# Thirty-five inner tiles of three feed-forward halves made with seven half-size products in place of eight

## The chip, the cores and the metric

The kernel runs on one core of one Trainium2 chip, in a single launch. The metric is the device time of an execution in microseconds, the median of three runs. All inputs come from the chip's memory, and packing of the inputs on the host is not timed.

## The reference, cut to what matters

A two-layer transformer over two token streams of 256 tokens each: a context stream and a latent stream, 1024 features. Each layer has a feed-forward half, a mixer (recurrence, two kinds of attention) and a second feed-forward half. A feed-forward half is, with 2816 inner features,

```
n   = rms_norm(h) * scale + shift            # 1024 features, scale and shift from a product with w_mod
gu  = n @ w_in                               # 2 x 2816: gate and up
h   = h + 0.5 * g * ((silu(gate) * up) @ w_out)
```

It is done for both streams with the same weights (each stream has its own scale, shift and g), except that the last layer's second half is done for the latent stream alone. So there are three halves over 512 tokens and one over 256. The vectors scale, shift and g come from w_mod (1024 x 9216 per layer) times a vector per stream. All is float32.

## The kernel before, in words

**Products.** Features lie on the 128 partitions, tokens along the free axis: x is eight tiles of 128 x 512, columns 0 to 255 the context, 256 to 511 the latents. To keep float32 precision, each operand is split in a high part in the rounded type fp32r and a low part (the rest), and a product is three matmuls: high by high, high by low, low by high (`mm3`, L625, its matmuls on L628 to L630). The normalised input is held in XH and XL.

**Weights.** All weights are packed by the host in the order of use into chunks of eight 128 x 128 blocks (128 x 1024, 512 KB; `plan`, L54). `loader` (L606) brings a chunk into a `raw` buffer (3 of them); ScalarE makes the high part (`split_hi`, L334) and VectorE the low part (`split_lo`, L340) into a pair of the `ring` (5 pairs). A raw buffer is free after the low part, a ring pair after the chunk's last matmul.

**A feed-forward half** (`ffn`, L813). There are 22 inner tiles f of 128 features. For each, gate and up are made over 8 tiles of k: 16 blocks, each three matmuls of 512 columns, into two PSUM banks (L898 to L905). `evac` (L825) then gives SiLU of gate on ScalarE (L830), the product with up on VectorE (L834), and the split of the result on ScalarE and VectorE (L846, L857). The first two or three tiles are made together, k by k, while the input is still being normalised. Inner tiles are taken in two groups of 11 (`GF`): after a group, `contract` (L908) multiplies its 11 tiles by w_out for each of the eight output tiles, three matmuls of 512 columns for each pair, and VectorE adds the result to x (`add_out`, L804, once for each stream).

**The modulation vectors.** While a feed-forward half runs, VectorE also forms the next scales, shifts and gates as dot products: `gemv` (L670) fetches 128 rows of w_mod (512 KB into a `graw` buffer, 6 of them) and takes two dot products over 1024 elements (L680, with an accumulator read behind each). `pump` (L702) lets a given number (`rates`) of them into the queue after each inner tile and output tile.

**The order of the work.** Every engine's instruction order is written out when the kernel is built. `Weave` (L362) is a planner: each piece of work is a step with an engine, a cost, buffers that it takes and gives, events that it waits for and an urgency; the planner always places the step that can start first, and of those within a small slack the one with the smallest urgency number. Dot products have urgency 90 (`U_GEMV`), the weight splits 18 (`U_W`), the evacuation of inner tiles 12 (`U_EVAC`). On the chip each engine follows its list in order and waits for the semaphores of what it needs. The lists `RANK`, `START`, `INPUTS` and `ORDER` set urgencies and order in the two mixers and at the start of the kernel, where the first scales and shifts are made by dot products (L1707) and small matmuls (L1691) from rows fetched in the order of `INPUTS`.

Of the kernel before, what the change touches and what calls it, by code (L numbers as in the profile page):

```python
# [17 lines left out]
try:  # L18
# [11 lines left out]
KT = 8  # L30
NF = FF // 128
GF = NF // 2
EPS = 1e-6
CH = 8
# [5 lines left out]
ORDER = ((("lx", 1), ("ukv", 0), ("nq", 0), ("nv", 0), ("lx", 2), ("cq", 0), ("cq", 1),  # L40
# [12 lines left out]

def plan():  # L54

    out = []

    def ffn(l, w):
        first = 3 if (l, w) == (0, 1) else 2
        for k in range(KT):  # L60
            out.extend((("fi", l, w, f, up, k), 1) for f in range(first) for up in range(2))
        for g in range(2):
            for f in range(max(first, g * GF), (g + 1) * GF):
                for up in range(2):
                    out.extend((("fi", l, w, f, up, k), 1) for k in range(KT))
            for dts in out_tiles(l, w):
                out.extend((("fo", l, w, dt, f), 1) for f in range(g * GF, (g + 1) * GF) for dt in dts)
# [24 lines left out]
def uses(key):  # L92

    kind, l = key[0], key[1]
    lat = l == L - 1
    if kind == "fi":
        _, _, w, f, _, _ = key
        return 2 if f < 2 and (l, w) != (0, 1) and not (lat and w == 2) else 1
    if kind == "fo":
        _, _, w, dt, f = key  # L100
        return 2 if f >= GF and dt >= KT - NORM_DT["ffn"] and not (lat and w == 2) else 1
# [26 lines left out]
def pack_weights(a):  # L128
    def block(key):
        kind, l = key[0], key[1]  # L130
        if kind == "fi":
            _, _, w, f, up, k = key
            m = a["ffn%d_w_in" % w][l]
            return m[k * 128:(k + 1) * 128, up * FF + f * 128:up * FF + (f + 1) * 128]
        if kind == "fo":
            _, _, w, dt, f = key
            return a["ffn%d_w_out" % w][l][f * 128:(f + 1) * 128, dt * 128:(dt + 1) * 128]
# [166 lines left out]
class Stream:  # L304
# [36 lines left out]

    def get(self, key):
# [19 lines left out]
class Weave:  # L362
# [62 lines left out]
    def run(self):  # L425
        while self.programs:
# [36 lines left out]
U_W, U_MAIN, U_EVAC, U_GEMV = 18, 50, 12, 90  # L463
N_POOL = 6
RANK = ({"ckv": 19.2, "conv": (-2, 47.5, 37.5), "nk": (-0.7, 19), "nv": 2.5, "cq": 16.9,
         "nq": (23, 10.2), "values": 72.2, "keys": (8, 17, 43.6),
         "query": (35.2, 45.9, 4.5, 18.5, 4.2, 11.8), "lru": (40, 40, 41), "gelu": (25, 22, 29),
         "att": (31, 11, 24.9, 17, 35), "evac": (50.4, 13.4, 5.8, 14.5, 32.1),
         "pv": (18.5, 13.5, 26.5, 34.1, 21.5), "main": 50},
        {"ckv": 48.7, "conv": (8, 38, 29), "nk": (36.5, 19.1), "nv": 43.7, "cq": 14.1, "nq": (7, 2),  # L470
         "values": 61.7, "keys": (18, 10, 19), "query": (9.5, -2.5, 10.5, 8.5, 7.7, 43.8),
         "lru": (40, 40, 43), "gelu": (16.8, 9.5, 32), "att": (25.6, 4, 2, 8, 49.2),
         "evac": (14, 23, 48.5, 17, 45.2), "pv": (9.5, 26.5, 8.5, 12.5, 13.5), "main": 50})
U_WNEXT, N_NEXT = 20, 9
START = {"scale": (1, 11, 5, 24.5, 29.2, 3, 9, 16),
         "shift": (24.6, 9.8, 8, 13, 29.8, 41.6, 14, 6.6),
         "apply": (0.5, 0.6, -1.5, -5.5, -5.5, -5.5, 1.5, -6.5)}
INPUTS = (("x", 1), ("x", 0), ("x", 2), ("cst",), ("x", 3), ("x", 4), ("x", 5), ("x", 6), ("x", 7),
          ("cols",), ("mod", 0, 0), ("weights", 1), ("mod", 1, 0), ("weights", 0), ("mod", 0, 1),
          ("mod", 1, 2), ("mod", 1, 1), ("mod", 0, 2), ("mod", 1, 3), ("weights", 2), ("mod", 0, 7),  # L480
          ("mod", 0, 3), ("mod", 1, 4), ("mod", 0, 5), ("mod", 0, 4), ("weights", 3), ("weights", 5),
          ("weights", 4), ("mod", 1, 5), ("mod", 0, 6), ("mod", 1, 6), ("mod", 1, 7))
# [4 lines left out]
def emit(tc, xT, cc, wmod, wst, cols_d, cst_d, nab, gates, wm0, ccol, out, layers=L):  # L487
# [3 lines left out]
    with es:  # L491
# [5 lines left out]
        raw = pool("raw", 3)  # L497
        ring = pool("ring", 5)
# [7 lines left out]
        w = Weave(dict(mm=3, sc=2, tr=2, o=1, ring=5, raw=3, nsq=2, nt=2), W)  # L506
# [104 lines left out]
        def split_hi(cs):  # L611
            for c in cs:
                yield S("ACT", act(W.size(c)), lambda: W.split_hi(c), take={"ring": 1},
                        wait=[("raw", c)] + ([("hi", c - 1)] if c else []), fire=("hi", c))

        def split_lo(cs):
            for c in cs:
                n = W.size(c)
                yield S(("DVE", "POOL") if c < N_POOL else ("DVE",), (dve(n), 2.3), lambda e=None: W.split_lo(
                    c, G if e == "POOL" else V), wait=[("hi", c)], give={"raw": 1}, fire=("chunk", c))  # L620

# [24 lines left out]
        def open_ffn():  # L646
            st = ph["st"] = ExitStack()
            ph["h"] = pool("ffnh", GF, st)
            ph["t"] = pool("ffnt", 2, st)
            ph["g"] = pool("gemv", 6, st)  # L650
            ph["g1"] = pool("gemv1", 1, st)
            now = w.clock["PE"]
            for tag, n in (("hp", GF), ("sg", 2), ("h", 2), ("graw", 6)):
                w.free[tag] = [now] * n
            ph["n"] = ph.get("n", 0) + 1
            if queue and ph["n"] > 1:
                w.spawn(U_GEMV - 1, silu_c(), now)
# [44 lines left out]
        def pump(n):  # L702
            for _ in range(min(n, len(queue))):
# [109 lines left out]
        def ffn(l, ww, p, streams, nxt, rates, start):  # L813
# [63 lines left out]

            if not both:
                w.spawn(1, rows(), w.clock["PE"])

# [16 lines left out]
            for grp in range(2):  # L897
                for f in range(max(done, grp * GF), (grp + 1) * GF):  # L898
# [7 lines left out]
                fs = range(grp * GF, (grp + 1) * GF)  # L906
# [45 lines left out]
        def mixer(l, p):  # L952
# [354 lines left out]
            def both_heads(a, s, i, evs, last):  # L1307
# [12 lines left out]
                yield S("PE", 1.4 * keys / 512, score, take={"sc": 2}, wait=[("nk", j), ("nq", j)] + evs["s"],  # L1320
# [292 lines left out]
        def startup():  # L1613
# [11 lines left out]

            def fetch(c, k):
                def f():
                    r = rows[c, k] = ph["g"].tile([128, 1024], F32, name="graw")
                    nc.sync.dma_start(r, wm0[ON_PE.index((c, k))] if (c, k) in ON_PE else wmod[0, c * 8 + k])
                return load(1024, f, take={"graw": 1}, fire=("wm", c, k))  # L1630

            def inputs():
                yield load(16, lambda: nc.sync.dma_start(sil[:, :, :2], ccol), fire="sil0")
                for s in range(2):
                    def row():
                        crow.append(ph["g"].tile([128, 1024], F32, name="graw"))
                        nc.sync.dma_start(crow[s][:1, :], cc[s * 1024:(s + 1) * 1024].unsqueeze(0))
                    yield load(3, row, take={"graw": 1}, fire=("crow", s))
# [19 lines left out]
            def wide(s, i):  # L1658
# [6 lines left out]
                yield S("PE", 0.86, copies, idle=True, take={"mm": 1}, give={"graw": 1} if i else {}, wait=[("crow", s)])  # L1665
# [16 lines left out]
            def product(c, k):  # L1682
# [13 lines left out]
                yield S("PE", 0.67, prod, idle=True, take={"sc": 1}, give={"graw": 1}, wait=[("wm", c, k), "sil"])  # L1696
# [6 lines left out]
            def dots(c, k):  # L1703

                m = mod[0, c][:, :, k]
                for s in range(2):
                    yield S("DVE", 1.14, lambda: V.scalar_tensor_tensor(  # L1707
                        ph["junk"], rows[c, k], 1.0, ph["sc"][:, s, :], OP.mult, OP.mult, accum_out=m[:, s:s + 1]),
                        wait=[("wm", c, k), ("silc", ph["n"], s)], give={"graw": 1} if s else {})
# [46 lines left out]
        def main():  # L1756
# [3 lines left out]
            yield from ffn(0, 1, 0, (0, 1), (0, 3), (2, 1), True)  # L1760
# [5 lines left out]
            yield from ffn(0, 2, 2, (0, 1), (1, 0), (2, 1), False)  # L1766
# [3 lines left out]
            yield from ffn(1, 1, 3, (0, 1), (1, 3), (2, 1), False)  # L1770
# [34 lines left out]
```

## Time and profile before

| what | value |
|---|---|
| median of 3 runs | 1765.95 us (1765.78 to 1766.14) |
| the profiled execution's own time | 1765.4 us |
| its span in the trace | 1763.6 us |
| PE busy / DVE busy / ACT busy | 1729.3 / 1194.7 / 694.9 us |
| bytes read from memory | 249.10 MB |

PE is TensorE's matmuls, PEld its weight loads, DVE VectorE, ACT ScalarE, POOL GpSimd, SPq the queue from which all transfers are issued. Matmuls are pipelined, and each record is longer than the distance to the next start; so the pace of a stream is read from starts, not from durations. A VectorE record likewise reaches some 0.08 us into the next one when the engine has no gap.

### The profile page before, as it was taken

What the parts mean: (1) busy time and instruction counts of PE and PEld (TensorE: products, weight loads), DVE (VectorE), ACT (ScalarE), POOL (GpSimd) and SP (SyncE); (2) the same over time, 40 slices, a digit from 0 to 9 for tenths busy, and PEclk for the clock granted to TensorE, in tenths of its full rate; (3) what the DMA queues carried; (4) which work ended last, traced back from release to release, by engine and by line L of the source; (5) the groups of instructions that cost most, each with busy time, mean ns of one, the idle gap of its engine ahead of it and who ended that gap; (6) DMA issues with size and microseconds to landing.
All of it is one profiled execution on the core that took longest, in us unless ns stands there. A gap on an engine that the chain in (4) does not pass through costs nothing.

```text
span 1763.6 us, 24185 instructions
## 1 busy us (share of the span) xinstructions
PE 1729.3 (98%) x9508; PEld 1428.9 (81%) x9508; DVE 1194.7 (68%) x1960; ACT 694.9 (39%) x1092; POOL 83.5 (5%) x70
## 2 busy tenths in 40 slices
PE   7999999999999999999999999999999999899999
PEld 4788888889766798888888898888888976599999
DVE  6898677636778678776775488765334577777564
ACT  4432122224777653222222242212222377754442
POOL 1100000000111010000000100000000111110000
PEclk9999999999999999999999999999999999999999
DMA  8565455322221126554553255543222232145554
GB/s 321 194 202 179 167 180 189 136 93 92 76 72 52 37 96 230 188 179 155 191 191 114 101 179 191 188 161 140 96 96 96 77 98 78 60 143 181 182 183 123
DMA packets 73591, 251.74 MB, mean 143 GB/s; under 512 B 9090, under 2 KB 12418, under 8 KB 73220
## 3 DMA queue, kind: packets, MB, share of 16 engines
q1 hardware_dynamic: 73476, 250.18, 41.4%
q8 instruction: 75, 1.23, 0.3%
q14 instruction: 40, 0.33, 0.1%
HBM read 249.10 MB, written 1.05 MB: 142 GB/s over the span
## 4 chain that ended last, share of the span: by engine, by line
PE 92%; DVE 4%; ACT 2%; issue 1%; POOL 0%; DMA 0%; SPq 0%; POOLq 0%; ACTq 0%; DVEq 0%
PE mm L628 27%; PE mm L629 27%; PE mm L630 27%; PE tr L1274 1%; PE sc L1298 1%; PE o L1351 1%; PE mm L1413 1%; DVE junk L1707 1%; PE o L628 1%; PE o L630 1%; PE o L629 1%; PE sc L1008 1%; PE tr L949 1%; PE sc L1316 1%; PE sc L628 0%
## 5 line engine op out<-in xcount | busy, mean ns | idle before, releaser
L628 PE MATMUL mm<-xh,whi 128*128 128x512 f32 (+2 forms) x1722 | 625.4, 363 | 8.7 <-DVE xh L990 5.2
L629 PE MATMUL mm<-xl,whi 128*128 128x512 f32 (+2 forms) x1722 | 613.8, 356 | 0.8 <-DVE xl L771 0.8
L630 PE MATMUL mm<-xh,wlo 128*128 128x512 f32 (+2 forms) x1722 | 613.3, 356 | 0.0
L334 ACT CAST whi<-wraw 128x1024 fp32r<-128x1024 f32 (+1 forms) x316 | 330.4, 1046 | 667.9 <-PE mm L629 458.9
L340 DVE TENSOR_TENSOR wlo<-wraw,whi 128x1024 fp32r<-128x1024 f32 (+1 forms) x311 | 379.5, 1221 | 256.2 <-ACT whi L334 253.3
L628 PEld LDWEIGHTS mm<-xh,whi 128*128 128x128 f32 x1722 | 326.4, 190 | 66.3 <-issue 6.9
L629 PEld LDWEIGHTS mm<-xl,whi 128*128 128x128 f32 x1722 | 326.4, 190 | 52.0 <-issue 2.6
L630 PEld LDWEIGHTS mm<-xh,wlo 128*128 128x128 f32 x1722 | 326.1, 189 | 50.6
L680 DVE SCALAR_TENSOR_TENSOR junk<-graw,silc 128x1024 f32<-128x1024 f32 x256 | 312.7, 1221 | 6.6 <-DMA graw<-in_wmod_dram 2.2
L628 PE MATMUL mm<-hh,whi 128*128 128x512 f32 (+1 forms) x748 | 264.5, 354 | 0.0
L629 PE MATMUL mm<-hl,whi 128*128 128x512 f32 (+1 forms) x748 | 263.2, 352 | 0.0
L630 PE MATMUL mm<-hh,wlo 128*128 128x512 f32 (+1 forms) x748 | 262.5, 351 | 0.0
L628 PEld LDWEIGHTS mm<-hh,whi 128*128 128x128 f32 x748 | 140.7, 188 | 21.3
L630 PEld LDWEIGHTS mm<-hh,wlo 128*128 128x128 f32 x748 | 140.4, 188 | 21.6
L629 PEld LDWEIGHTS mm<-hl,whi 128*128 128x128 f32 x748 | 140.8, 188 | 20.5
L804 DVE SCALAR_TENSOR_TENSOR x<-mm,mod,x 128x256 f32<-128x256 f32 x158 | 71.2, 479 | 86.0 <-PE mm L630 85.5
L846 ACT CAST hh<-h 128x512 fp32r<-128x512 f32 (+1 forms) x88 | 49.6, 567 | 158.1 <-DVE h L834 133.8
L834 DVE TENSOR_TENSOR h<-sg,mm 128x512 f32<-128x512 f32 x62 | 42.5, 686 | 69.8 <-PE mm L630 69.1
L857 DVE TENSOR_TENSOR hl<-h,hh 128x512 fp32r<-128x512 f32 (+1 forms) x88 | 54.5, 623 | 33.9 <-ACT hh L846 33.7
L723 POOL TENSOR_TENSOR acc<-acc,nsq 128x256 f32<-128x256 f32 x20 | 20.5, 1023 | 1097.3 <-ACT nsq L719 1097.3
L743 POOL TENSOR_TENSOR rr<-rv,nhalf 128x2 f32<-128x2 f32 (+2 forms) x29 | 37.8, 1308 | 289.8 <-DVE rv L736 212.7
L719 ACT ACTIVATE nsq<-x 128x256 f32<-128x256 f32 x63 | 25.5, 415 | 62.2 <-DVE x L804 62.2
(240 smaller groups left out, 1508.1 us busy)
## 6 DMA issues: line engine op xcount, KB each, us to landing
wraw<-in_wst_dram SPq DMA_DIRECT2D x308, 512.0 KB, 3.5
graw<-in_wmod_dram SPq DMA_DIRECT2D x137, 512.0 KB, 5.2
graw<-in_wm_dram SPq DMA_DIRECT2D x7, 512.0 KB, 7.2
x<-in_xT_dram SPq DMA_DIRECT2D x8, 256.0 KB, 5.0
nab<-in_nab_dram SPq DMA_DIRECT2D x16, 128.0 KB, 2.1
silc<-in_cc_dram SPq DMA_DIRECT2D x2, 1024.0 KB, 5.9
m_gw<-in_gates_dram SPq DMA_DIRECT2D x6, 256.0 KB, 3.6
out_dram<-x SPq DMA_DIRECT2D x8, 128.0 KB, 1.9
```

The source lines that it names most:

```text
L334: self.nc.scalar.copy(hi[:, :n], self.raws[i][:, :n])
L340: eng.tensor_tensor(lo[:, :n], self.raws.pop(i)[:, :n], hi[:, :n].bitcast(F32), OP.subtract)
L628: PE.matmul(o, wh[:, :m], h, start=start, stop=False)
L629: PE.matmul(o, wh[:, :m], lo, start=False, stop=False)
L630: PE.matmul(o, wl[:, :m], h, start=False, stop=stop)
L680: V.scalar_tensor_tensor(ph["junk"], g["r"], 1.0, ph["sc"][:, s, :], OP.mult, OP.mult, accum_out=mod[l, c][:, s, j:j + 1])
L719: A.activation(t, x[:, dt, half(s)], AF.Square)
L743: G.tensor_tensor(r, v, e, OP.pow)
L804: yield S("DVE", 0.4, lambda: V.scalar_tensor_tensor(x[:, dt, half(s)], o[:, half(s)], gate[:, s, dt:dt + 1], x[:, dt, half(s)], OP.mult, ...
L834: V.tensor_tensor(g["h"][:, cs], g["s"][:, cs], pu[:, cs], OP.mult)
L846: A.copy(hs[f][0][:, cs], g["h"][:, hc])
L857: yield S("DVE", dve(n), lambda: V.tensor_tensor(hs[f][1][:, cs], g["h"][:, hc], hs[f][0][:, cs].bitcast(F32), OP.subtract), give={"h": 1} ...
```

## The change

In 35 of the 66 inner tiles of the three halves over both streams, gate and up are made by the Winograd form of a two by two block product. The weights of a tile are the blocks gate and up by k 0 to 3 and k 4 to 7; the input's blocks are k 0 to 3 and k 4 to 7 by context and latents. Seven products of half-size blocks (four k tiles, 256 columns) take the place of eight. Each product is 4 k tiles by three matmuls of 256 columns. The tiles: `DIRECT` gives the first such f of each half, 13, 12 and 6; so 9, 10 and 16 tiles.

- **Weights of such a tile** (`seven`): its two chunks hold the four blocks (`sa`, `sb`). VectorE forms four sums of blocks over 512 elements, and of the seven resulting operands ScalarE makes the high parts (three over 512 elements, two over 1024) and VectorE the low parts (the same five). They lie in three ring pairs and a half-size pair (`half`); one scratch tile `sx`.
- **Input sums** (`sums_of_x`, `last_sum`): once for each half, six sums and three splits over 1024 elements, and for each of four k tiles three sums and a split over 256. The last of them overwrites a quarter of XH and XL when the plain tiles are done. Two `graw` buffers and `sx` serve as scratch.
- **Products** (`fast`, `fasts`): products 1, 5, then 3 of the tile before, 6, 2, 4 of the tile before, 7; at the end of a group 3 and 4 of its last tile. They accumulate in quarters of three PSUM banks.
- **Evacuation** (`evac7`): ScalarE copies three partial results (256 columns), applies SiLU twice (256) and makes the high part (512); VectorE adds twice, multiplies twice (256 each) and makes the low part (512).
- **Groups**: the three halves have three groups of inner tiles (8, 7, 7) in place of two of 11; the fourth half keeps two of 11.
- **Buffers**: raw 3 to 4, ring 5 to 6, graw 6 to 2 in the three halves; the rows for the start lie in a pool of their own (`graw0`, 6) that is closed before the input sums.
- **Lists**: `RANK`, `START`, `INPUTS`, `ORDER` and the numbers of `pump` (`RATES`, now fractions) have other values; the planner's cost of the scores of one mixer step is another; `dynamic_dma_scratch_size=1024` is given.

```diff
-GF = NF // 2
+GROUPS = {(0, 1): (0, 8, 15, 22), (0, 2): (0, 8, 15, 22), (1, 1): (0, 8, 15, 22), (1, 2): (0, 11, 22)}
+DIRECT = {(0, 1): 13, (0, 2): 12, (1, 1): 6, (1, 2): 22}
...
+URG = {'seven': 16.7, 'evac7': -10.7, 'sums': (24.4, 52.7, 10.8), 'last': 4.6}
+RATES = ((4.11, 1.93, 2.03), (2.3, 0.51, 2.05), (1.04, 0.93, 1.42))
...
-        raw = pool("raw", 3)
-        ring = pool("ring", 5)
+        raw = pool("raw", 4)
+        ring = pool("ring", 6)
...
+                yield S("ACT", act(512), open_a, take={"ring": 1}, wait=[("raw", c), ("hi", c - 1) if begins else
+                                                                         other(-1, "openC")], fire=ev("openA"))
+                yield S("DVE", dve(512), lambda: lo("A", a, raw(0, a)), fire=ev("A11"))
+                yield S("DVE", dve(512), s3, take={"sx": 1})
+                yield S("DVE", dve(512), s1, wait=[("raw", c + 1)], fire=ev("s1"))
+                yield S("DVE", dve(512), lambda: tt(g["x"][:, b], raw(0, b), raw(0, a), OP.subtract), fire=ev("s2"))
...
+                yield S("ACT", act(1024), open_c, take={"ring": 1}, wait=[] if begins else [other(-1, "openB")],
+                        fire=ev("openC"))
+                yield S("DVE", dve(1024), lambda: lo("C", whole, g["x"]), wait=[ev("s4")], give={"sx": 1},
+                        fire=ev("C"))
...
+                yield S("DVE", dve(512), lambda: tt(raw(0, a), raw(1, b), g["x"][:, b], OP.subtract), fire=ev("s4"))
+                yield S("ACT", act(512), lambda: hi("A", b, raw(0, b)))
+                yield S("DVE", dve(512), lambda: lo("A", b, raw(0, b)), fire=ev("S1"))
+                yield S("ACT", act(512), open_d, take={"half": 1})
+                yield S("DVE", dve(512), lambda: lo("D", a, raw(0, a)), give={"raw": 1}, fire=ev("D"))
...
+                yield S("ACT", act(1024), open_b, take={"ring": 1}, wait=[ev("s1"), ev("openC") if ends else
+                                                                          other(1, "openA")], fire=ev("openB"))
...
+                yield S("DVE", dve(1024), lambda: lo("B", whole, raw(1, whole)), give={"raw": 1}, wait=[ev("s4")],
+                        fire=ev("B"))
...
+            P7 = {1: ("A", 0, "X", ["A11"]), 6: ("C", 1, "X", ["C"]), 7: ("C", 0, "X", []), 4: ("B", 0, "X", []),
+                  5: ("A", 1, "Q", ["S1"]), 3: ("D", 0, "Q", ["D"]), 2: ("B", 1, "Y", ["B"])}
...
+                    PE.matmul(o, wh, xh, start=n in (1, 5) and k == 0, stop=False, **on)
+                    PE.matmul(o, wh, xl, start=False, stop=False, **on)
+                    PE.matmul(o, wl, xh, start=False, stop=k == 3, **on)
...
+                for k in range(4):
+                    yield S("PE", 0.328, lambda: go(k), wait=(ws if k == 0 else []) + ([("T", p, 4, k)] if n == 4 else []),
...
+                for n in (1, 5, -3, 6, 2, -4, 7):
+                    if n > 0:
+                        yield from fast(f, n)
+                    elif prev is not None:
+                        yield from fast(prev, -n)
+                if f == run[-1]:
+                    yield from fast(f, 3)
+                    yield from fast(f, 4)
...
+                    yield S("DVE", dve(256), tt(("h", qb), ("h", qb), ("X", qa), OP.add), wait=[ev(7)],
+                            fire=ev("C22"))
+                    yield S("DVE", dve(256), tt(("sg", qb), ("sg", qb), ("Q", qa), OP.add), wait=[ev(3)],
+                            give={"tr": 1})
+                    yield S("ACT", act(256), silu(("sg", qb), ("sg", qb)), table="silu")
+                    yield S("DVE", dve(256), tt(("h", qb), ("sg", qb), ("h", qb), OP.mult), fire=ev("lat"))
...
+                    yield S("DVE", dve(256), tt(("h", qa), ("sg", qa), ("X", qa), OP.mult),
+                            wait=[ev(4), ev("C11")], give={"mm": 1})
+                    yield S("ACT", act(512), hi, take={"hp": 1}, wait=[ev("lat")], give={"sg": 1})
...
-            yield from ffn(0, 1, 0, (0, 1), (0, 3), (2, 1), True)
+            yield from ffn(0, 1, 0, (0, 1), (0, 3), RATES[0], True)
```

## Rows read from the trace of the kernel before

**Rows 1.** The page's busy times: engine, busy us (share of the span), instructions.

```profile
PE 1729.3 (98%) x9508; PEld 1428.9 (81%) x9508; DVE 1194.7 (68%) x1960; ACT 694.9 (39%) x1092; POOL 83.5 (5%) x70
```

**Rows 2.** Windows by stage: us, then each engine's busy us and records, clock, DMA.

```profile
0.00:64.00 64.00, 49.35 (x256) 33.53 (x257) 50.46 (x80) 28.98 (x61) 15.86 (x11) 0.97 0.68 248
64.00:416.00 352.00, 352.00 (x1586) 287.15 (x1586) 249.72 (x398) 103.10 (x136) 5.46 (x6) 1.00 0.48 166
416.00:640.00 224.00, 220.34 (x1365) 165.84 (x1364) 158.95 (x314) 140.35 (x261) 22.78 (x18) 1.00 0.20 67
...
656.00:1020.00 364.00, 364.00 (x1688) 298.92 (x1687) 252.77 (x377) 103.72 (x140) 5.32 (x6) 1.00 0.47 166
1020.00:1380.00 360.00, 360.00 (x1654) 294.93 (x1653) 208.88 (x299) 99.45 (x132) 3.66 (x3) 1.00 0.41 142
1380.00:1590.00 210.00, 197.44 (x1418) 162.62 (x1418) 156.28 (x314) 136.30 (x247) 26.18 (x24) 0.98 0.29 92
1590.00:1763.60 173.60, 170.13 (x1418) 169.91 (x1417) 103.47 (x150) 71.52 (x94) 0.00 (x0) 1.00 0.53 168
```

**Rows 3.** Waits of PE, longest first: line, whom it waited for, us, times, longest.

```profile
PE mm L628 <- DVE xh L990: 5.2, 1, 5.2
PE tr L1274 <- ACT m_p L1262: 4.5, 6, 1.9
PE sc L751 <- DVE h L1722: 4.2, 1, 4.2
```

**Rows 4.** ACT's timeline, 1060 to 1180 us: start, us, line, operation; four consecutive SiLUs.

```profile
1091.92 0.59 ACT L830 ACTIVATE sg<-mm 128x512 f32<-128x512 f32 x1
...
1103.16 0.58 ACT L830 ACTIVATE sg<-mm 128x512 f32<-128x512 f32 x1
...
1114.40 0.59 ACT L830 ACTIVATE sg<-mm 128x512 f32<-128x512 f32 x1
...
1125.65 0.59 ACT L830 ACTIVATE sg<-mm 128x512 f32<-128x512 f32 x1
```

**Rows 5.** PE's timeline, 419 to 425.5 us: matmuls of 256 columns, first and 49th.

```profile
419.23 0.28 PE L628 MATMUL mm<-xh,whi 128*128 128x256 f32 x1
...
424.92 0.28 PE L628 MATMUL mm<-xh,whi 128*128 128x256 f32 x1
```

**Rows 6.** Groups by line, weight loads: count, busy us, mean ns, idle before.

```profile
L628 PEld LDWEIGHTS mm<-xh,whi 128*128 128x128 f32 x1722 | 326.4, 190 | 66.3 <-issue 6.9 <-DVE xh L990 6.0 <-ACT xh L770 3.0
```

**Rows 7.** DVE's timeline, 1060 to 1180 us: consecutive instructions without gap, and an `add_out`.

```profile
1063.89 1.23 DVE L340 TENSOR_TENSOR wlo<-wraw,whi 128x1024 fp32r<-128x1024 f32 x1
1065.03 0.68 DVE L857 TENSOR_TENSOR hl<-h,hh 128x512 fp32r<-128x512 f32 x1
1065.63 1.22 DVE L680 SCALAR_TENSOR_TENSOR junk<-graw,silc 128x1024 f32<-128x1024 f32 x1
1066.78 0.08 DVE L680 DVE_READ_ACCUMULATOR junk<-graw,silc 128x1 f32 x1
1066.89 1.22 DVE L680 SCALAR_TENSOR_TENSOR junk<-graw,silc 128x1024 f32<-128x1024 f32 x1
...
1163.45 0.88 DVE L804 SCALAR_TENSOR_TENSOR x<-mm,mod,x 128x256 f32<-128x256 f32 x2 [0.37 <-PE mm L630]
```

**Rows 8.** DVE's timeline, 1600 to 1650 us: two consecutive reads of PSUM.

```profile
1604.81 0.42 DVE L838 TENSOR_TENSOR sg<-mm,R 128x257 f32<-128x257 f32 x1
1605.14 0.41 DVE L838 TENSOR_TENSOR h<-mm,R 128x257 f32<-128x257 f32 x1
```

**Rows 9.** The whole timeline, 1120 to 1150 us: the end of one tile's evacuation.

```profile
1129.18 0.69 DVE L834 TENSOR_TENSOR h<-sg,mm 128x512 f32<-128x512 f32 x1 [1.02 <-PE mm L630]
...
1129.89 0.62 ACT L846 CAST hh<-h 128x512 fp32r<-128x512 f32 x1 [3.65 <-DVE h L834]
...
1130.55 0.69 DVE L857 TENSOR_TENSOR hl<-h,hh 128x512 fp32r<-128x512 f32 x1 [0.69 <-ACT hh L846]
```

**Rows 10.** DMA issues: count, KB each, median us from issue to landing.

```profile
wraw<-in_wst_dram SPq DMA_DIRECT2D x308, 512.0 KB, 3.5
graw<-in_wmod_dram SPq DMA_DIRECT2D x137, 512.0 KB, 5.2
```

More of the change, by code (lines that the diff above doesn't have):

```diff
@@ L51, in out_tiles, with groups @@
     return ((0, 1),) + tuple((dt,) for dt in range(2, KT)) if (l, w) == (L - 1, 2) else tuple((dt,) for dt in range(KT))
+def groups(l, w):
+    g = GROUPS[l, w]
+    return [range(a, b) for a, b in zip(g, g[1:])]
 def plan():
@@ L505, in emit @@
         W = Stream(nc, wst, raw, ring)
-        w = Weave(dict(mm=3, sc=2, tr=2, o=1, ring=5, raw=3, nsq=2, nt=2), W)
+        w = Weave(dict(mm=3, sc=2, tr=2, o=1, ring=6, raw=4, nsq=2, nt=2), W)
         def mmt():
@@ L876, in rows, with quarter, sums_of_x, f32 @@
                 yield S("ACT", actp(256), lambda: A.copy(R[:, :256], g["R"][:, :256]), give={"tr": 1}, fire=("R", p))
+            us = dict(zip(((0, 1), (0, 2), (1, 1)), URG["sums"])).get((l, ww))
+            def quarter(ks, s):
+                return tuple(t[:, 4 * ks:4 * ks + 4, half(s)] for t in (XH, XL))
+            def sums_of_x():
+                B11, B12, B21, B22 = (quarter(i, j) for i in range(2) for j in range(2))
+                def f32(t):
+                    return t.bitcast(F32)
+                r = {}
+                T = []
+                def tt(o, a, b, op, **k):
+                    def go():
+                        if not T:
+                            ph["start"].close()
+                            tp = pool("t7", 1, ph["st"])
+                            T.extend([tp.tile([128, 4, 256], F32R, name="t7%s%d" % (n, i)) for n in "hl"]
+                                     for i in range(3))
+                            ph["T"] = T
+                        if o not in r:
+                            t = ph["sx"].tile([128, 1024], F32, name="sx") if o == 3 else \
+                                ph["g"].tile([128, 1024], F32, name="graw")
+                            r[o] = t.rearrange("p (a b) -> p a b", a=4)
+                        x0, x1 = (r[i] if isinstance(i, int) else f32(i) for i in (a, b))
+                        V.tensor_tensor(r[o], x0, x1, op)
+                    return S("DVE", dve(1024), go, **k)
+                def split(i, h, lo, ev, give):
+                    yield S("ACT", act(1024), lambda: A.copy(h, r[i]))
+                    yield S("DVE", dve(1024), lambda: V.tensor_tensor(lo, r[i], f32(h), OP.subtract), fire=ev,
+                            give={"graw": 1} if give else {})
+                new = {"graw": 1}
+                yield tt(1, *B12, OP.add, wait=[("xin", p, s, k) for s in range(2) for k in range(KT)], take=new)
+                yield tt(2, *B22, OP.add, take=new)
+                yield tt(3, 2, 1, OP.subtract, take={"sx": 1})
+                yield from split(3, *T[2], ("T", p, 3), False)
+                yield tt(3, *B11, OP.add)
+                yield tt(1, 1, 3, OP.subtract, give={"sx": 1})
+                w.spawn(us, split(1, *T[0], ("T", p, 1), True), w.clock["DVE"])
+                yield tt(2, 2, 1, OP.subtract)
+                yield from split(2, *T[1], ("T", p, 2), True)
+                for k in range(4):
+                    w.spawn(URG["last"], last_sum(k))
@@ new lines, in last_sum, with part @@
+            def last_sum(k):
+                g, (h, lo) = {}, quarter(0, 1)
+                def part(i):
+                    g[i] = nrm.tile([128, 256], F32, name="nt")
+                    V.tensor_tensor(g[i], *(t[i][:, k, :].bitcast(F32) for t in (quarter(1, 0), ph["T"][1])), OP.subtract)
+                yield S("DVE", dve(256), lambda: part(0), wait=[("direct", p)], take={"nt": 1})
+                yield S("DVE", dve(256), lambda: part(1), take={"nt": 1})
+                yield S("DVE", dve(256), lambda: V.tensor_tensor(g[0], g[0], g[1], OP.add), give={"nt": 1})
+                yield S("ACT", act(256), lambda: A.copy(h[:, k, :], g[0]))
+                yield S("DVE", dve(256), lambda: V.tensor_tensor(lo[:, k, :], g[0], h[:, k, :].bitcast(F32), OP.subtract),
+                        give={"nt": 1}, fire=("T", p, 4, k))
@@ new lines, in ffn, with seeded, go @@
+            qa, qb = slice(0, 256), slice(256, 512)
+            P7 = {1: ("A", 0, "X", ["A11"]), 6: ("C", 1, "X", ["C"]), 7: ("C", 0, "X", []), 4: ("B", 0, "X", []),
+                  5: ("A", 1, "Q", ["S1"]), 3: ("D", 0, "Q", ["D"]), 2: ("B", 1, "Y", ["B"])}
+            yb, st7 = [], {}
+            def seeded():
+                def go():
+                    u = S7[l, ww, DIRECT[l, ww]]["A"][0]
+                    yb.append(ot())
+                    PE.matmul(yb[0][:, qa], u[:, :128], XH[:, KT - 1, half(0)], start=True, stop=True)
+                yield S("PE", 0.11, go, take={"o": 1}, give={"o": 1}, wait=[("s7", l, ww, DIRECT[l, ww], "openA")])
@@ L896, in ffn @@
             done = len(tags) // 2
-            for grp in range(2):
-                for f in range(max(done, grp * GF), (grp + 1) * GF):
+            gs = groups(l, ww)
+            for grp, fs in enumerate(gs):
+                grp = grp == len(gs) - 1
+                for f in fs:
+                    if f == DIRECT[l, ww]:
+                        w.at["direct", p] = w.clock["PE"]
+                    if f >= DIRECT[l, ww]:
+                        if f == DIRECT[l, ww]:
+                            yield from seeded()
+                        if f == fs[-1] and grp:
+                            pump(len(queue))
+                        yield from fasts(f, fs)
+                        pump(rates[2])
+                        continue
+                    if f < done:
+                        continue
+                    if f == fs[-1] and grp:
+                        pump(len(queue))
                     bag = {}
@@ L1695, in keep @@
                     A.copy(g["r"][:, :128], g["o"][:, :128])
-                yield S("PE", 0.67, prod, idle=True, take={"sc": 1}, give={"graw": 1}, wait=[("wm", c, k), "sil"])
+                yield S("PE", 0.67, prod, idle=True, take={"sc": 1}, give={"graw0": 1}, wait=[("wm", c, k), "sil"])
                 yield S("ACT", 0.2, keep, take={"nt": 1})
```

227 lines of the change are left out of this document (189 added, 38 removed), and 6 rows, old and new, of the table ORDER.

## The prediction, made before the result

> **What bounds the kernel now.** I read the page's busy times first [rows 1]: PE is busy 98% of the span, DVE 68%, ACT 39%. That mean hides stages, so the next view is the windows by stage [rows 2]. In the three feed-forward halves over both streams (64 to 416, 656 to 1020, 1020 to 1380 us) PE is busy for every microsecond of the window, although DVE too shows 250 of 352, 253 of 364 and 209 of 360 us. PE is idle only at the start (14.65 us), in the first mixer (3.66) and in the second (12.56); the 3.5 us of the last window are the tail. The waits of PE [rows 3] say the same: the longest is 5.2 us, and its lines lie in the mixers and the start, none in a feed-forward half. So in the stretches that change, time is the number of matmuls by their pace, and any column taken away shortens the kernel, as long as the other engines keep up with less time for each tile.
>
> **What is removed on PE.** A plain inner tile is 48 matmuls of 512 columns. Three consecutive ones take 1125.65 - 1091.92 = 33.73 us between the SiLUs of the first and the fourth [rows 4]: 11.24 us a tile, 234.2 ns a matmul. A new tile is 7 products by 4 k tiles by 3 = 84 matmuls of 256 columns. Matmuls of that size, with as many weight loads as matmuls, run in the first mixer: 48 of them from 419.23 to 424.92 us [rows 5], 118.5 ns each. So a new tile takes 84 x 118.5 = 9.96 us and saves 1.29 us; 35 of them save **45.0 us**. A narrow matmul costs 1.2% more for each column than a wide one, which takes 0.1 us of each tile and is in the sum. The three matmuls that seed a bank (one for each half) add 0.4 us at most.
>
> The Trainium skill's page "TensorE: Matmul & The Clock Gate" (Back-to-back issue gap) puts the distance of warm matmuls at columns / 2.4 GHz plus 2.5 ns, so 215.8 and 109.2 ns. This trace does not agree with the size: 234.2 and 118.5 ns at a granted clock of 1.00. By the page a tile would save 1.19 us and all of them 41.5 us; by the rows 45.0.
>
> **What is added on DVE.** Its pace is read from starts without a gap [rows 7]: a split of 1024 elements 1.14 us (1063.89 to 1065.03), an operation over 512 0.60 us (1065.03 to 1065.63), a dot product with its accumulator read 1.26 us (1065.63 to 1066.89), so 2.52 us for a `gemv`; an operation over 256 takes 0.33 us [rows 8], an `add_out` of two streams 0.88 us with its overlap, 0.80 without [rows 7].
> - A plain tile costs DVE 2 splits of 1024 and 2 operations of 512: 3.48 us of 11.24.
> - A new tile costs 4 block sums of 512 and 3 low parts of 512 (7 x 0.60), 2 low parts of 1024 (2.28), and in the evacuation 4 of 256 and 1 of 512 (1.92): 8.40 us of 9.96, that is 84%.
> - The input sums are 9 operations of 1024 and 16 of 256: 10.3 + 5.3 = 15.6 us for each half. The third group adds 8 x 0.80 = 6.4 us for each half.
>
> So DVE gets 9, 10 or 16 times 4.92 us, and 22 us more in each half: 66, 71 and 101 us. Against the halves' busy time of before, with the 0.08 us by which a record overlaps the next taken off [rows 2], this makes 218 + 66 = 284 of 340 us, 223 + 71 = 294 of 351, and 185 + 101 = 286 of 339 us: 83 to 84% (91 to 93% if the overlap is left in). All of it fits beside PE. ACT gets some 2 us for each new tile on 28 to 30% and is no bound.
>
> **Where it could still wait.** The sum fits, but not in every stretch. A new tile leaves DVE 1.56 us, six tenths of a `gemv`, while the new rates let in 2.05 and 1.42 for each new tile of the second and third half (in the first, 8 x 4.11 + 8 x 1.93 have let in all 48 before the first new tile). They have urgency 90 against 16.7 of the splits and -10.7 of the evacuation, so in the written lists they slide to the `contract` stretches: seven tiles by 8 by 3 matmuls of 512 columns are 39.4 us, in which DVE needs 7 x 1.14 + 6.4 = 14.4 us and has room for ten. The places in which no row shows a wait, with their bounds:
> - *End of a group of new tiles* (7 of them). After product 7, product 3 (12 matmuls, 1.42 us) is all that lies before product 4, which needs an addition of 0.33 us on DVE; behind one dot product that is 1.6 us and a release, 0.5 us late. Then the last tile's evacuation (about 2.0 us by the chain in [rows 9]) has six other tiles' matmuls, 4.2 us, before its result is asked for. Bounds 0 and 0.7 us each; I take 0.4, together 3.
> - *First new tile of a half* (3). Its operands need 6.5 us of DVE in a row, and a ring of six pairs lets them be made about one tile ahead. Bounds 0 and 6.5 us; nearest is a plain tile, which leaves DVE 7.8 us, so I take 1 each, together 3.
> - *The steady run of new tiles.* Bounds 0 (DVE at 84%) and 0.5 us a tile (one dot product in front of a late split, once in two or three tiles); I take 1 us in all, since these halves show no PE idle at all at their DVE load of before [rows 2].
> - *Transfers.* Each weight chunk lands 3.5 us after issue and a `graw` row 5.2 us [rows 10]. With 2 buffers two rows need 5.2 + 2.5 us or more, so 48 of them need 185 us of 340: hidden. But all transfers are issued in order by SP, and a row that waits for its buffer holds the chunk behind it; four raw buffers are two tiles of cover. Bounds 0 and 10 us; I take 0.
> - *Start and mixers.* Their lists are others, with the same transfers and products. The idle time there is 30.9 us in all [rows 2]; another order of the same work could take off or add some 6 us. I take 0, and keep -6 to +6.
>
> The profiled execution took 1765.4 us (span 1763.6 and 1.8 around it), 0.55 below the median of the runs. 1765.4 - 45.0 + 0.4 + 7 = 1727.8, so **1728 us** as a median.
>
> **The rivals.**
> 1. *DVE holds the new tiles in part.* The splits come late behind dot products and waiting evacuations, DVE's list being strictly in order. For it: 84% without any `gemv`, and preparation only one tile ahead. Against: PE did not wait in the stretches where DVE was fullest. If each new tile takes 10.5 us in place of 9.96, 19 us of the gain go: 1746.
> 2. *DVE is the bound, and the kernel is slower.* If the lists place the dot products among the new tiles at the rate at which they are let in, a new tile takes 8.40 + 2.05 x 2.52 = 13.57 us in the second half, 8.40 + 1.42 x 2.52 = 11.98 in the third and, by its rate, 13.5 in the first: against 11.24, 10 x 2.33 + 16 x 0.74 + 9 x 2.3 = 56 us more: 1821. It decides from (11.24 - 8.40) / 2.52 = 1.13 dot-product pairs in front of each tile's splits. Against it stand their urgency and the room in `contract`.
> 3. *The full gain, with better lists at the start and in the mixers.* No new waits, 4 us off the idle: 1717.
> 4. *Narrow matmuls that pay for their weight loads.* A load is recorded with 190 ns [rows 6], and there are 84 in place of 48 for each tile; 36 more in series are 6.8 us against 1.29 saved, +194 us: 1960. The change would then not give what its count says. Against: 118.5 ns is the distance between starts with a load for each matmul [rows 5, 6]. The Trainium skill's page "TensorE: Matmul & The Clock Gate" (What overlaps and what doesn't) says that a load overlaps a running matmul only if their row groups differ, which would make this the outcome; the trace speaks against it, since these loads use all rows and are hidden.
>
> **How the numbers follow.** Forecast (1720 to 1738): 0.70. Rival 1 (1738 to 1762): 0.15. Rival 3: 0.09. Rival 2: 0.04. Rival 4: 0.01. The remaining 0.01 is a loss at the start and in the mixers that eats the gain. What a measurement of this kernel can tell from no change is about 0.2%, 3.5 us. Faster: the forecast, rivals 3 and nearly all of 1, 0.93; within 0.2%: 0.02; slower: 0.05. The range takes rival 3 and half of rival 1: 1717 to 1746.
>
> **What would show it.** The PE matmuls over T sums and weight units should have starts 118 to 119 ns apart, and new tiles in a run should follow each other by 9.9 to 10.2 us (distance of the high-part casts of consecutive tiles). Waits of PE for weight splits or for the additions of the evacuation should be under 10 us over the three halves, most at ends of groups. DVE should show over 90% busy by records there. The forecast is wrong if new tiles follow at over 10.5 us, if PE in the halves waits for SP's transfers, or if the start or a mixer moves by over 6 us.

## The result: 1710.8 us, 55 us faster, and the profile after

The changed kernel takes 1710.79 us (median of 4 runs, 1709.51 to 1712.87) against 1765.87: a ratio of 0.9689, 95% interval 0.9672 to 0.9706. Forecast were 1728 us and a range of 1717 to 1746. The sign was right and most of the gain comes from where it was forecast, but the time lies below the range, and the missing part is not in the feed-forward halves.

The page's busy times of the changed kernel, to be read against [rows 1]: 48 us less of PE, 233 us more of DVE, at the same 98% for PE.

```profile
PE 1681.8 (98%) x10699; PEld 1456.3 (85%) x10699; DVE 1427.6 (83%) x2436; ACT 805.2 (47%) x1348; POOL 95.1 (6%) x77
```

Where the time went is seen when both executions are cut at the same events: the last `add_out` of each stage. The windows of the kernel before, with the columns of [rows 2] (rows: the first 80 us, the rest of the first half, first mixer, second half, third half, second mixer):

```profile
0.00:80.00 80.00, 65.35 (x318) 46.31 (x319) 63.85 (x102) 36.97 (x73) 15.86 (x11) 0.96 0.70 254
80.00:412.40 332.40, 332.40 (x1494) 270.77 (x1493) 232.82 (x367) 92.93 (x120) 4.68 (x4) 1.00 0.46 161
412.40:645.90 233.50, 229.84 (x1446) 175.34 (x1445) 168.35 (x337) 146.51 (x276) 26.23 (x21) 1.00 0.22 73
645.90:1016.50 370.60, 370.60 (x1744) 305.52 (x1743) 257.57 (x389) 108.45 (x148) 6.05 (x6) 1.00 0.47 164
1016.50:1389.20 372.70, 372.70 (x1761) 307.63 (x1760) 218.74 (x322) 107.16 (x147) 6.04 (x6) 1.00 0.40 138
1389.20:1569.80 180.60, 168.79 (x1180) 134.17 (x1179) 135.60 (x280) 120.16 (x224) 21.67 (x20) 0.97 0.28 88
```

And of the changed kernel:

```profile
0.00:80.00 80.00, 65.79 (x320) 47.67 (x321) 65.23 (x104) 38.15 (x75) 13.31 (x10) 0.94 0.68 244
80.00:402.90 322.90, 321.39 (x1794) 277.52 (x1793) 296.12 (x491) 121.76 (x188) 13.42 (x9) 1.00 0.57 175
402.90:633.80 230.90, 229.81 (x1444) 175.68 (x1444) 170.60 (x343) 145.72 (x274) 26.50 (x21) 1.00 0.21 70
633.80:994.50 360.70, 358.68 (x2082) 313.47 (x2081) 323.75 (x523) 141.70 (x224) 15.00 (x11) 1.00 0.53 169
994.50:1347.20 352.70, 352.12 (x2313) 320.95 (x2312) 316.93 (x524) 158.01 (x266) 3.05 (x4) 1.00 0.46 148
1347.20:1517.00 169.80, 164.35 (x1179) 131.75 (x1178) 138.28 (x289) 118.19 (x218) 20.79 (x20) 1.00 0.29 91
```

The second number of each row is its length. The halves lost 9.5, 9.9 and 20.0 us, 39.4 together, of which 0.4 belong to the start (the same inner tile's SiLU comes at 124.66 in place of 125.03 us): 39.0 without them. The mixers lost 2.6 and 10.8, 13.4 together; the last half is the same within 0.3 us. These are 52.8 us. The profiled execution was the slowest of the four (1712.87), and the median holds some 2 us more, probably at the start: that SiLU comes at 121.7 to 124.7 us in seven other kernels with the new order at the start, and at 125.0 to 126.0 in the six with the old.

### The profile page after: what moved, and what is told of

The parts are those of the page before. It is cut to its first block, busy times and chain, and to the rows that moved or that the text cites. A ratio compares the mean times of both kernels' runs of the same rounds, so it can differ in the third digit from the quotient of the medians.

```text
span 1711.1 us, 27422 instructions
## 1 busy us (share of the span) xinstructions
PE 1681.8 (98%) x10699; PEld 1456.3 (85%) x10699; DVE 1427.6 (83%) x2436; ACT 805.2 (47%) x1348; POOL 95.1 (6%) x77
## 3 DMA queue, kind: packets, MB, share of 16 engines
HBM read 249.10 MB, written 1.05 MB: 146 GB/s over the span
## 4 chain that ended last, share of the span: by engine, by line
PE 87%; DVE 7%; ACT 2%; issue 2%; POOL 0%; DMA 0%; SPq 0%; POOLq 0%; ACTq 0%; DVEq 0%
PE mm L763 19%; PE mm L764 19%; PE mm L765 19%; PE mm L1118 4%; PE mm L1120 4%; PE mm L1119 4%; PE tr L1120 2%; PE tr L1119 2%; PE tr L1118 2%; DVE junk L820 1%; PE o L1678 1%; PE tr L1601 1%; PE sc L1625 1%; PE o L1120 1%; PE o L1119 1%
## 5 line engine op out<-in xcount | busy, mean ns | idle before, releaser
L763 PE MATMUL mm<-xh,whi 128*128 128x512 f32 (+2 forms) x1162 | 405.2, 349 | 2.3 <-ACT xh L913 1.0
L764 PE MATMUL mm<-xl,whi 128*128 128x512 f32 (+2 forms) x1162 | 391.7, 337 | 3.7 <-DVE xl L914 2.3
L765 PE MATMUL mm<-xh,wlo 128*128 128x512 f32 (+2 forms) x1162 | 391.1, 337 | 0.0
L355 DVE TENSOR_TENSOR wlo<-wraw,whi 128x1024 fp32r<-128x1024 f32 (+1 forms) x242 | 295.5, 1223 | 79.6 <-ACT whi L349 78.3
L763 PEld LDWEIGHTS mm<-xh,whi 128*128 128x128 f32 x1162 | 220.5, 190 | 36.4 <-issue 9.1
L764 PEld LDWEIGHTS mm<-xl,whi 128*128 128x128 f32 x1162 | 220.8, 190 | 31.2 <-issue 3.8
L765 PEld LDWEIGHTS mm<-xh,wlo 128*128 128x128 f32 x1162 | 220.4, 190 | 25.0
L692 ACT CAST whi<-wraw 128x512 fp32r<-128x512 f32 (+1 forms) x105 | 79.0, 764 | 135.2 <-PE mm L764 97.2
L686 DVE TENSOR_TENSOR wlo<-wraw,whi 128x512 fp32r<-128x512 f32 (+1 forms) x105 | 90.0, 865 | 4.7 <-ACT whi L692 4.6
L1120 PE MATMUL mm<-t7h,wlo 128*128 128x256 f32 x280 | 79.1, 283 | 0.0
```

The lines of the kernel that those rows point to most:

```text
L355: eng.tensor_tensor(lo[:, :n], self.raws.pop(i)[:, :n], hi[:, :n].bitcast(F32), OP.subtract)
L686: V.tensor_tensor(o, x0, x1, op)
L692: A.copy(g[u][0][:, h], src)
L763: PE.matmul(o, wh[:, :m], h, start=start, stop=False)
L764: PE.matmul(o, wh[:, :m], lo, start=False, stop=False)
L765: PE.matmul(o, wl[:, :m], h, start=False, stop=stop)
```

## The experiments

Stage lengths, from the last `add_out` of one stage to that of the next (us; the first column is the end of the first half from the span's start):

| kernel | median | 1st half ends | 1st mixer | 2nd half | 3rd half | 2nd mixer |
|---|---|---|---|---|---|---|
| before | 1765.9 | 412.4 | 233.5 | 370.6 | 372.6 | 180.6 |
| changed | 1710.8 | 402.9 | 230.8 | 360.7 | 352.8 | 169.8 |
| a_plain | 1761.7 | 412.9 | 230.4 | 370.7 | 372.5 | 181.0 |
| a_dots | 1709.6 | 400.5 | 230.7 | 360.3 | 352.8 | 169.9 |
| a_start | 1718.0 | 401.9 | 237.1 | 360.8 | 352.8 | 169.5 |
| a_mixold | 1717.1 | 400.0 | 233.2 | 361.3 | 352.2 | 172.8 |
| a_rank1 | 1716.0 | 401.0 | 230.9 | 360.8 | 352.8 | 175.2 |
| a_score | 1714.2 | 400.2 | 234.6 | 360.7 | 352.8 | 169.1 |
| a_less6 | 1723.9 | 403.6 | 230.4 | 364.3 | 359.6 | 169.5 |
| a_more6 | 1731.0 | 400.4 | 239.8 | 359.6 | 364.1 | 169.5 |
| b_mixnew | 1756.6 | 413.1 | 231.2 | 370.7 | 372.7 | 175.5 |
| b_ring | 1763.5 | 413.2 | 233.3 | 370.7 | 372.7 | 177.7 |
| b_fill | 1769.3 | 413.4 | 233.5 | 370.7 | 372.7 | 184.4 |
| b_fill2 | 1763.4 | 413.1 | 233.2 | 370.7 | 372.7 | 178.8 |

Kernels named a_ are the changed kernel with an edit, b_ the kernel before with one.

**The mixers' lists undone, and done alone.** Theory 1 is the lists, theory 2 the larger buffers, theory 3 that they only fit each other.

```diff
a_mixold:  RANK, ORDER and the cost of the score step as before
a_rank1:   RANK of layer 1 as before
b_mixnew:  RANK, ORDER and the cost of the score step as changed
b_ring:    raw 3 -> 4, ring 5 -> 6, dynamic_dma_scratch_size=1024
```

> The changed kernel with the mixers' lists of before (RANK, ORDER and the planner's cost of the score step), all else as changed. Theory 1 (the lists alone made the mixers 2.6 and 10.8 us shorter): both mixers go back, 1711 + 13 = 1724 us, with PE idle of about 12 us and two dips of the clock in the second mixer. Theory 2 (the larger weight buffers, ring 6 and raw 4, did it): no change, 1711 us. Theory 3 (lists and buffers only fit each other): worse than either, over 1726 us.

> The changed kernel with the second mixer's urgencies alone as before (RANK of layer 1). Theory 1: the second mixer loses its 10.8 us, 1722 us; the first keeps its 2.6. Theory 2: 1711 us. Theory 3: over 1724 us.

> The kernel before with the new mixers' lists (RANK, ORDER, cost of the score step) and nothing else of the change. Theory 1: the gain comes without any of the new products, 1766 - 13 = 1753 us. Theory 2: 1766 us. Theory 3: 1766 us or slower, up to 1776.

> The kernel before with the ring of six pairs and four raw buffers (and the smaller scratch that makes room for them), its lists and products as before. Theory 1: no change, 1766 us within 4. Theory 2: the second mixer is some 10 us shorter, 1753 us. Theory 3: 1766 us or slower.

Ratios to the kernel before: 0.9727 (0.9712 to 0.9741), 0.9718 (0.9702 to 0.9734), 0.9951 (0.9936 to 0.9966), 0.9986 (0.9976 to 0.9995). None of the three theories holds alone. The lists take 8.9 us off the kernel before without any new product (theory 1 said 13), and undoing them costs the changed kernel 6.3, not 13. In a_rank1 the second mixer loses half of its 10.8 us, 5.4. The buffers, with the smaller scratch, are worth 2 to 3 us alone, in the second mixer. The first mixer takes 231 us with the new lists and 233 with the old in these four; further runs below, which have the new lists too, take 230 to 240 us.

**No new tiles.**

```diff
-DIRECT = {(0, 1): 13, (0, 2): 12, (1, 1): 6, (1, 2): 22}
+DIRECT = {(0, 1): 22, (0, 2): 22, (1, 1): 22, (1, 2): 22}
```

> The changed kernel with no tile made from seven products (DIRECT 22 in all halves; no block sums, no input sums); its groups, buffers and lists as changed. Theory A (35 x 1.24 us less some 4 us of new waits is what the seven products give; the rest of the 55 us comes from the second mixer, the first and the start): the second half takes 370 to 371 us and the third 372 to 373, as before, and the whole 1711 + 39 = 1750 us, within 5 for the mixers' order. Theory B (the products give nearly all): 1711 + 53 = 1764 us.

It takes 1761.7 us, ratio 0.9976 (0.9966 to 0.9985): 12 us above theory A and near theory B, for a reason that neither had. The halves are back at 370.7 and 372.5 us as theory A said, so the tiles' own gain, with their waits, is 39 to 40 us. But the second mixer too is back, at 181.0 us, with the new lists and the new buffers. Its windows row against the changed kernel's last row above: 3.6 us more busy and 7.6 more idle.

```profile
1386.40:1567.40 181.00, 167.94 (x1180) 133.00 (x1179) 137.39 (x288) 121.41 (x222) 21.13 (x20) 0.99 0.28 86
```

**One number of the planner; another order at the start; two tiles more or fewer.**

```diff
a_score:   S("PE", 0.18 + 0.775 * keys / 512, ...) -> S("PE", 1.4 * keys / 512, ...)
a_start:   START and INPUTS as before
a_more6:   DIRECT 11, 10, 4
a_less6:   DIRECT 15, 14, 8
```

> The changed kernel with one number of the planner as before: the cost that it puts down for a score step of the mixers (the work and every list are as changed). Theory (the written order of a mixer follows from everything that the planner counted before it, so its length moves by several us with any such number, and the lists were found for one state of it): the mixers together take 3 to 12 us more than 400.6 us, by other waits, the halves the same: 1714 to 1723 us. Rival (the new urgencies alone make the second mixer short): 1711 us, the second mixer within 1 us of 169.8.

> The changed kernel with START and INPUTS, the order at the start, as before. Theory: the new order at the start gives about 2 us: 1713 us, first add_out 2 us later, mixers within 3 us as they are. Rival (the start is as long as before and only run-to-run differences show): 1711 us.

> The changed kernel with two more new tiles in each of the three halves (DIRECT 11, 10 and 4; 41 of 66). Theory (PE still sets the pace of a half): each half 2.5 us shorter, 358.2 and 350.3 us for the second and third, within 1; the mixers some us longer, since their lists were found for another state. Rival (VectorE is at its end with 9, 10 and 16): the halves no shorter, or longer.

> The changed kernel with two new tiles less in each half (DIRECT 15, 14 and 8; 29 of 66). Theory: each half 2.5 us longer, 363.2 and 355.3 us for the second and third, within 1, and the mixers some us longer. If the waits of the second half come from too many new tiles, it is less than 2.5 us longer.

Ratios 0.9710, 0.9730, 0.9805 and 0.9764, each within 0.0016. a_score moved the first mixer by 3.7 us and the second by 0.7 the other way, at the lower end of what was expected. a_start costs 7.2 us, but not as expected: its first `add_out` comes 3.3 us later than in the profiled execution of the changed kernel (139.3 in place of 136.0), yet the first half ends 1 us earlier, and 6.3 us are in the first mixer, at whose start PE waits 4.0 us for sums of squares and reciprocal roots on POOL. In a_start, a_more6 and a_less6 the second mixer's written order is the changed kernel's (over 99% of the instructions of PE, DVE and ACT stand in the same sequence), and it takes 169.5 us in all three; in a_plain, counted by operation and tiles, only 56% of DVE's do. So where the written order is the same, the second mixer's length is the same, and that order hangs on what the planner counted ahead of it: a_plain has the changed kernel's lists and buffers and another order. Which of its rules makes the two orders differ is not settled.

The two slopes were a miss: 41 and 29 new tiles are both slower than 35. In a_less6 the second half is 3.6 us longer (2.5 expected), the third 6.9. In a_more6 the second half gains 1.1 us, the first mixer loses 9.0 and the third half 11.3, the last by these waits of PE (line, whom it waited for, us, times, longest):

```profile
PE tr L899 <- POOL rr L886: 3.4, 2, 2.6
PE tr L1120 <- DVE wlo L686: 3.2, 1, 3.2
PE sc L894 <- POOL acc L866: 2.7, 1, 2.7
```

The second is product 5 of the half's third new tile, which waits for the low part of its operand. It costs 2.5, 2.8 and 3.2 us in the three halves of a_more6 and 2.5 in the first and third of a_less6, always at the third new tile. With the chosen `DIRECT` it is 0.6 us, in the second half alone:

```profile
831.05 0.39 PE L1120 MATMUL tr<-t7h,wlo 128*128 128x256 f32 x1 [0.56 <-DVE wlo L686]
```

In the first and third half of the changed kernel, and in the second of a_less6, the products with w_out of a group lie ahead of the third new tile, and none of them has this wait. The other two waits of a_more6 stand at 1000 to 1007 us, in the normalisation that begins the third half; its first mixer has 5.7 us of the same kind. VectorE has dot products left there, but no run tests whether these are the cause.

**Shorter dot products.** Lines as in the changed kernel, over 128 of the 1024 elements.

```diff
-    V.scalar_tensor_tensor(ph["junk"], g["r"], 1.0, ph["sc"][:, s, :], OP.mult, OP.mult,
+    V.scalar_tensor_tensor(ph["junk"][:, :128], g["r"][:, :128], 1.0, ph["sc"][:, s, :128], OP.mult, OP.mult,
```

> The changed kernel with the dot products of the halves over 128 elements in place of 1024 (the modulation vectors are then other numbers; the order of every engine is the same). Theory A (the 2 to 4 us that the first and second half lose against 9 and 10 times 1.24 us are VectorE late at their ends behind dot products): the second half takes 358 to 359 us in place of 360.7, the first 1 to 2 us less, the third no less; the whole 1707. Rival (the waits are the chain of the normalisation itself, or the splits): no change in any half, 1711 us.

1709.6 us, ratio 0.9682 (0.9668 to 0.9697), no different from the changed kernel. From the SiLU named above to its end the first half is 1.2 us shorter, as theory A said; the second half is 0.4 us shorter, not 2, and the third is the same. So the dot products cost the halves little. The changed kernel's trace shows 1.9 us of waits of PE in the second half, of which the first went in a_dots and the others stayed:

```profile
PE sc L894 <- POOL acc L866: 0.9, 1, 0.9
PE tr L1120 <- DVE wlo L686: 0.6, 1, 0.6
PE tr L899 <- POOL rr L886: 0.4, 1, 0.4
```

**Matmuls in a wait.** The second mixer of before loses more than it idles: 168.8 us of PE busy against 164.4 for the same matmuls.

```diff
 b_fill:   at the first output tile's first block
+                            for _ in range(18):
+                                PE.matmul(g["o"], u[:, :128], u[:, :512], start=True, stop=True)
 b_fill2:  at its third block
+                            for _ in range(34):
+                                PE.matmul(g["o"][:, cs], zero, u[:, :256], start=False, stop=False)
```

> The kernel before with 18 matmuls of 512 columns, whose result is overwritten, put in front of the matmul of the second mixer that waits 5.2 us at 1536.7 us. Theory (PE comes out of that wait at half its clock and loses some 2.7 us more): the granted clock stays 1.00 from 1531 to 1542 us, the matmuls behind the wait follow at 119 in place of 210 ns, the second mixer takes 178 in place of 180.6 us, the whole 1763. Rival (the clock has no part in it): 1766 us.

> The kernel before with 34 matmuls of 256 columns by a tile of zeros (they add nothing) directly in front of the third block of the second mixer's first output tile, the matmul that waits 5.2 us; they run inside the wait (the first try put 18 wide ones at the first block, 16 us ahead of the wait, where they cost 4.3 us). Theory (PE comes out of the wait at half its clock and loses some 2.7 us): the granted clock stays 1.00 behind the wait, the 256-column matmuls there follow at 119 in place of 210 ns, the second mixer takes 178 in place of 180.6 us. Rival (the clock has no part in it): 180.6 us or more by what of the filler outlasts the wait.

b_fill took 1769.3 us, ratio 1.0022 (1.0013 to 1.0031): its matmuls stood 16 us ahead of the wait, at 1520.9 us, and cost their 4.3 us; the wait and the drop of the clock stayed. b_fill2 took 1763.4 us, ratio 0.9987 (0.9978 to 0.9997), with a second mixer 1.9 us shorter (2.7 expected) although it does 34 matmuls more. It has the smaller scratch too, but up to the wait it runs as before: the waiting matmul starts 147.5 and 147.6 us into the stage. PE's timeline of the kernel before:

```profile
1536.70 0.58 PE L628 MATMUL mm<-xh,whi 128*128 128x256 f32 x1 [5.19 <-DVE xh L990]
...
1537.75 0.41 PE L628 MATMUL mm<-xh,whi 128*128 128x256 f32 x1
1537.96 0.42 PE L629 MATMUL mm<-xl,whi 128*128 128x256 f32 x1
1538.17 0.42 PE L630 MATMUL mm<-xh,wlo 128*128 128x256 f32 x1
```

And of b_fill2:

```profile
1531.53 4.43 PE L1578 MATMUL mm<-whi,zero 128*128 128x256 f32 x34
1537.28 0.39 PE L632 MATMUL mm<-xh,whi 128*128 128x256 f32 x1 [1.32 <-DVE xh L994]
...
1538.09 0.28 PE L632 MATMUL mm<-xh,whi 128*128 128x256 f32 x1
1538.21 0.28 PE L633 MATMUL mm<-xl,whi 128*128 128x256 f32 x1
1538.33 0.28 PE L634 MATMUL mm<-xh,wlo 128*128 128x256 f32 x1
```

Behind an idle 5.2 us the starts are 0.21 us apart, the lower of the two clock levels; behind the filled wait 0.12. The granted clock of that stretch, by windows of before and then of b_fill2 (third column from the right), goes from 0.69 to 1.00:

```profile
1531.00:1542.00 11.00, 5.81 (x19) 3.91 (x18) 7.33 (x16) 3.89 (x8) 0.00 (x0) 0.69 0.00 0
```

```profile
1531.00:1541.00 10.00, 8.61 (x58) 6.77 (x55) 8.02 (x17) 4.60 (x9) 0.00 (x0) 1.00 0.01 2
```

The Trainium skill's page "TensorE: Matmul & The Clock Gate" (What's actually happening) says that the slow clock is what an idle engine falls back to and that activity releases it. By that rule a long wait on PE costs more than its length; this trace agrees, with 1.9 us on top of 5.2.

## Why the prediction was wrong, point by point

**PE's gain by tile: right.** It is read from ScalarE's copies of product 1 in consecutive new tiles (start, us, line, operation). In the last group of the third half they are 10.00 us apart, in the other groups mostly 9.88, as here in the second half. Forecast was 9.96.

```profile
900.23 0.36 ACT L1163 COPY o<-mm 128x256 f32<-128x256 f32 x1
...
910.11 0.36 ACT L1163 COPY o<-mm 128x256 f32<-128x256 f32 x1 [0.50 <-PE mm L1120]
...
919.99 0.36 ACT L1163 COPY o<-mm 128x256 f32<-128x256 f32 x1
```

```profile
1254.04 0.36 ACT L1163 COPY o<-mm 128x256 f32<-128x256 f32 x1
...
1264.04 0.36 ACT L1163 COPY o<-mm 128x256 f32<-128x256 f32 x1 [0.53 <-PE mm L1120]
...
1274.04 0.36 ACT L1163 COPY o<-mm 128x256 f32<-128x256 f32 x1
```

So a matmul of 256 columns takes 117.6 or 119.0 ns (118.5 forecast), and a tile saves 1.36 or 1.24 us (1.29). What chooses between the two paces is not known. For the 35 tiles this makes an estimate of some 46 us, against 45.0: 28 x 1.36 + 7 x 1.24 = 46.8, less 1 us because each of the seven groups begins slower, with 60 matmuls in 7.2 us. Weight loads stayed hidden with 84 for each tile: rival 4 is out.

**DVE beside PE: right.** It is busy for 296 of 323, 324 of 361 and 317 of 353 us by records, 92, 90 and 90% (forecast: over 90%), and PE's idle in those windows is 1.5, 2.0 and 0.6 us. Rivals 1 and 2 are out: new tiles follow at 10.00 us at most, and with hardly any dot products (a_dots) they follow at the same two paces.

**New waits: the size came out, the places did not.** The halves lost 39.0 us, some 7 short of that estimate, and 7 was forecast. But the trace shows only 3.7 us of it as waits of PE, and none at the ends of groups of new tiles or at a half's first new tile, which had 3 us each in the sum. 3.1 us are the normalisation at the end of the halves (1.2, 1.3 and 0.6), of which 2.5 wait for POOL: a cost for which the prediction had no term. 0.6 us are the third new tile of the second half; a_less6 and a_more6 show that this small price belongs to this `DIRECT` and not to the products. The other 3 us or so are found in no wait, and their cause stays open. That the sum of the halves came within 1 us is thus in part luck.

**Start and mixers: this step failed.** The sentence was "I take 0, and keep -6 to +6", on the reason that another order of the same work could move the 30.9 us of idle time by some 6. The mixers lost 13.4 us, 10.8 of them in the second, and these put the time below the range. (A mixer that moves by over 6 us was among the prediction's own signs of being wrong.) Two things were mis-sized. First, the second mixer's 12.56 us of idle time in [rows 2], 11.8 between its own bounds, were waits of a written order [rows 3], such as the one of 5.2 us for a copy on VectorE, so more than half could go at once: it idles 5.45 us now, and this is its longest wait:

```profile
PE mm L764 <- DVE xl L1813: 1.1, 1, 1.1
```

Second, the windows already showed that idle time was not its whole price, since the granted clock was 0.98 there; by finer cuts its PE is busy for 4.4 us less now for the same matmuls, at a clock of 1.00, and b_fill2 shows 1.9 of them behind one wait. Rival 3 (better lists in the mixers) came nearest, at 4 us and a chance of 0.09, but it is not the whole mechanism: the new lists alone make the second mixer 5.1 us shorter in b_mixnew and not at all in a_plain. What made the planner's order come out so well in the changed kernel stays open. The part of the sum on which all the working was spent missed by 1.0 us (45.0 − 7 = 38.0 us forecast, 39.0 measured); the part taken at 0 missed by 13.4.

## What to carry to other kernels

When a change comes with new lists for stages that it doesn't otherwise touch, bound those stages by all that they lose, idle time and slow clock, and not by a guess around zero. A half-width product nearly keeps its price for each column when weight loads hide (117.6 to 119.0 ns for 256 columns, 234.2 for 512), so on a kernel bound by TensorE seven products in place of eight pay, as long as VectorE has the time: here it is busy for 233 us more, 6.7 for each new tile. With an order written out by a planner, test a part alone by its stage's length and not by the whole time: any edit ahead of a stage can rewrite that stage.

## What the runs showed of the hardware that was not expected

At the end of the second half of the changed kernel, an addition over 256 elements on POOL and the dot products on DVE lengthen each other. DVE's timeline:

```profile
972.78 1.22 DVE L820 SCALAR_TENSOR_TENSOR junk<-graw,silc 128x1024 f32<-128x1024 f32 x1
973.93 0.08 DVE L820 DVE_READ_ACCUMULATOR junk<-graw,silc 128x1 f32 x1
974.05 1.64 DVE L820 SCALAR_TENSOR_TENSOR junk<-graw,silc 128x1024 f32<-128x1024 f32 x1
```

And POOL's, where the same addition takes 0.74 us at 995.61, with no dot product beside it:

```profile
972.88 1.72 POOL L866 TENSOR_TENSOR acc<-acc,nsq 128x256 f32<-128x256 f32 x1 [3.61 <-ACT nsq L862]
...
987.53 1.21 POOL L866 TENSOR_TENSOR acc<-acc,nsq 128x256 f32<-128x256 f32 x1 [0.46 <-ACT nsq L862]
...
995.61 0.74 POOL L866 TENSOR_TENSOR acc<-acc,nsq 128x256 f32<-128x256 f32 x1 [3.60 <-ACT nsq L862]
```

POOL's instruction at 972.88 starts 0.1 us into one dot product, ends 0.55 us into the next, and that one takes 0.42 us longer. a_dots shows that it is the dot products: beside ones over 128 elements the first four of these additions take 0.74 to 0.79 us in place of 1.66 to 1.72. The Trainium skill's page "SBUF — State Buffer" (Who interferes with whom) says that a DVE instruction with two SBUF inputs contends with a GpSimd instruction that reads SBUF, and that the ports which they share are an exclusive lock. The trace agrees: it looks like 1.05 us of waiting and 0.7 of work on POOL, then part of that work as a delay on DVE. On the path to the next stage lies the addition at 987.53: it takes 1.21 us, and PE then waits 0.9 us for it (the first wait of the list under the shorter dot products). In a_dots it takes 0.73 us, and PE does not wait for it:

```profile
984.60 0.73 POOL L866 TENSOR_TENSOR acc<-acc,nsq 128x256 f32<-128x256 f32 x1 [1.85 <-ACT nsq L862]
```
